# One plain tile of gate and up instead of two at the front of each feed-forward layer, with the sums of x chained

## The chip, the cores and the metric

The program runs on one core of one Trainium2 chip. The core has a matrix engine (TensorE, "PE" in the rows; "PEld" is its loading of the stationary operand), a vector engine (VectorE, "DVE"), a scalar engine (ScalarE, "ACT"), a general engine (GpSimd, "POOL") and a queue engine (SyncE, "SP"). Each takes its instructions in a fixed order that was settled when the program was built. The metric is the device time of one execution in microseconds. Before the change it is 2099.26 us, the median of 3 runs (2099.06 to 2102.05).

## The reference

Two residual layers over a (1, 1024, 1024) stream, every sub-layer behind an RMSNorm. The even layer mixes by a short convolution and an mLSTM, the odd layer by a gated MLP over chunks. Each of the two ends in a SwiGLU feed-forward with D_MODEL = 1024 and D_FF = 2816, and that is where the change lies:

```python
def swiglu(xn, w_in, w_out):
    h = xn @ w_in
    g, up = h[..., :D_FF], h[..., D_FF:]
    return (jax.nn.silu(g) * up) @ w_out

# in each layer
x = x + mixer(rmsnorm(x, norm_mix[layer]), ...)
x = x + swiglu(rmsnorm(x, norm_ffn[layer]), ffn_w_in[layer], ffn_w_out[layer])
```

## The kernel before

Activations lie transposed: 8 blocks d of 128 features by two halves c of 512 tokens, in float32. Every product is made in three passes of TensorE (`mm3`, L121 to L123): each operand is cut into a rounded part (h) and the remainder (l), and h·h, h·l and l·h are added up. A cut costs one cast on ACT (L96 for x, L110 or L329 for weights) and one subtraction on DVE (L97, L111, L330).

The hidden layer has NF = 22 tiles f of 128 features, each with a gate and an up part. They are computed in two ways.

- The first DIRECT = 2 tiles are **plain** (`direct`, L429 on): for each half c of the tokens `project` runs gate and up over all 8 blocks, 48 matmuls of 128x512 per tile and half. The tiles of PSUM are called f0g and f0u in layer 0, f1g and f1u in layer 1.
- The other tiles are made **by quarters** (`Halves`, `blocks`, `into`): the gate and up weights of a tile are one row of blocks a11, a12, a21, a22, x is cut into four blocks by feature half and token half, and seven products in the manner of Winograd replace eight. A unit is one tile; its seven products have 12 matmuls each, 84 in all, into three banks A, B and C of PSUM (Af0i, Bf0i, Cf0i). The order of the products is fixed in `STEPS`: a11·b11, a12·b21, s2·t2, s1·t1, s3·t3, s4·b22, a22·t4. The weights' own sums (s1 to s4, L340 to L343) come out of DVE and are cut as hix/lox (s2, s4), hiy/loy (s1, a22) and hiz/loz (s3); a11 and a12 are hia/loa.

On the side of x, b11 is feature blocks 0 to 3 of token half 0, b21 blocks 4 to 7 of half 0, and b22 blocks 4 to 7 of half 1; all three are there already as the cut x that the plain tiles use. The four sums t1 to t4 are not. They are made by adding DMAs on the POOL queue (`gather`, L394: the destination in SBUF is added to, 256 KB each, in place in the float32 x), four blocks each, `mix_x`, and then cut on ACT and DVE, `cut_x`. So there are 16 gathers per layer. In the names of the rows xe (layer 0) and xo (layer 1) is the float32 x; x_ffn01*k*h and x_ffn01*k*l is block k of token half 1 after scaling and cutting; f0t1*k*h is the rounded part of block k of t1.

The second half of x is not ready when the layer starts. The mixer's output projection ends with half 1; then TensorE sums the squares (ss_ffn, L162), DVE makes the root (L166 to L190) and a diagonal matrix of it (dg_ffn, L175), TensorE spreads that over the partitions (r_ffn, L179), ACT copies it to SBUF (L244), and DVE scales the eight blocks (L248), each of which is then cut (L96, L97). Only after the scaling of a block may a gather read it.

The program is written in one sequence; a list scheduler at build time decides from it, by priorities and its own costs, the order on each engine. Pools set limits: 4 staging buffers for weights (`wst`), 4 for the rounded and 4 for the remainder parts (`whl`), 5 + 3 banks of PSUM. The generator `blocks` loads and cuts the first unit's weights step by step, one step for each `next(run)`; the steps of `swiglu` that call it lie at L581 to L596.

Of the kernel before, what the change touches and what calls it, by code (L numbers as in the profile page):

```python
# [25 lines left out]
EPS = 1e-6  # L26
PAIRS = (2, 2, 2, 3)
TAIL = 4
DIRECT = 2
GELU_C = math.sqrt(2.0 / math.pi)  # L30
GELU_A = 0.044715
BIG = 1e30
# [11 lines left out]
def trunk(ctx, tc, x_t, vecs, b_gate, b_s, ws_t, we, we_v, we_g, we_o, wo_u, wo_v, wo_o, wf_in, wf_out, out_t):  # L44
# [48 lines left out]
    def split(src, name):  # L93
        hi = slot(f"{name}h", F32R)
        lo = slot(f"{name}l", F32R)
        nc.scalar.copy(hi[:, :HALF], src)  # L96
        nc.vector.tensor_tensor(lo[:, :HALF], src, hi[:, :HALF].bitcast(F32), op=ALU.subtract)  # L97
        return hi, lo
# [264 lines left out]
    def blocks(units):  # L363

        w = units[0][0]
        w.load()
        yield
        w.rows()
        yield
        w.sums()  # L370
        yield
        w.below()
        w.third()
        yield
        for i, (w, xb, sink, then) in enumerate(units):
            ahead = units[i + 1][0] if i + 1 < len(units) else None
            if ahead:
                ahead.load()
            banks = {"a": acc(f"A{w.name}"), "b": acc(f"B{w.name}"), "c": misc(f"C{w.name}")}
            for s, (wn, xn, bank, first) in enumerate(STEPS):  # L380
                wh, wl = w.get(wn)
                ps = banks[bank]
                nt = w.n // P
                for k in range(nt):
                    cols = slice(k * P, (k + 1) * P)
                    xh, xl = xb[xn][k]
                    mm3(ps, (wh[:, cols], wl[:, cols]), (xh[:, :HALF], xl[:, :HALF]), first and k == 0, k == nt - 1, not first)
                sink(s, ps)
                if ahead and s in (1, 4, 5, 6):
                    {1: ahead.rows, 4: ahead.sums, 5: ahead.below, 6: ahead.third}[s]()  # L390
                then(s)

    def gather(dst, src):
        nc.gpsimd.dma_start(dst, src, accum_op=ALU.add)  # L394

    def swiglu(layer, normed, todo, spans, after):
# [19 lines left out]
        def settle(f):  # L416

            if f >= NF - TAIL:
                for c in range(2):
                    store(hs.pop((f, c)), td[f - NF + TAIL], c, f"{name}h{f}{c}")  # L420
            elif f % 2:
                x11, x12, x21, x22 = (hs.pop((ff, c)) for ff in (f - 1, f) for c in range(2))
                for b, t in (("b11", x11), ("b21", x21), ("b22", x22)):
                    store(t, hd[f // 2], BLOCKS.index(b), f"{name}h{f}{b}")
                for b, t, more in (("t1", x11, x12), ("t3", x12, x22), ("t2", x22, x11), ("t4", x21, x22)):
                    nc.vector.tensor_tensor(t, t, more, op=ALU.add)
                    store(t, hd[f // 2], BLOCKS.index(b), f"{name}h{f}{b}")

        def direct(f):  # L429
            wg = weights(wf_in[layer, f], f"{name}g{f}")  # L430
            wu = weights(wf_in[layer, NF + f], f"{name}u{f}")

            def job(c):
                pg = project(wg, xs, c, f"{name}g{f}{c}")
                pu = project(wu, xs, c, f"{name}u{f}{c}")
                hs[f, c] = gate(pg, pu, f, c)

            return job

        def into(f):  # L440
            st = {}

            def sink(s, ps):
# [23 lines left out]
                else:  # L467
                    r = st["r"]
                    nc.vector.scalar_tensor_tensor(r, r, 0.5, ps, op0=ALU.mult, op1=ALU.mult)
                    hs[f, 0] = r  # L470
                    if f == DIRECT:
                        settle(f - 1)
# [11 lines left out]
        def onto(dp, ch):  # L484
            opening = ch == 0
            rows, hold = (2 * dp, 2 * dp + 1), {}

            def add(d, c, t):
                to = x[d][c][:, :HALF]
                nc.vector.tensor_tensor(to, t, to, op=ALU.add)  # L490

            def keep(d, c, ps):
                t = slot(f"{name}x{d}{c}" if opening else f"{name}e{d}{c}")
                if opening:
                    x[d][c] = t
                hold[d, c] = t[:, :HALF]
                nc.scalar.copy(hold[d, c], ps)

            def less(d, c, p, q):
                nc.vector.tensor_tensor(hold[d, c], p, q, op=ALU.subtract)  # L500
                if not opening:
                    gather(x[d][c][:, :HALF], hold[d, c])

            def sink(s, ps):
                d0, d1 = rows
                if s in (0, 6) and opening:
                    keep(d0 if s == 0 else d1, 0, ps)
                elif s in (0, 1, 6):
                    add(d1 if s == 6 else d0, 0, ps)
                elif s in (2, 3):  # L510
                    keep(d0 if s == 2 else d1, 1, ps)
                elif s == 4:
                    less(d1, 1, hold[d1, 1], ps)
                else:
                    less(d0, 1, ps, hold[d0, 1])
                if s == 6 and ch == len(PAIRS) - 1:
                    for d in rows:
                        for c in range(2):
                            gather(x[d][c][:, :HALF], x_in[d * P : (d + 1) * P, c * HALF : (c + 1) * HALF])

            return sink
# [19 lines left out]
        def early(ch, todo):  # L541
            def then(s):
                for i in todo.get(s, ()):
                    bring(ch, i)

            return then

        units, xb = [], {b: [] for b in BLOCKS}
        for f in range(DIRECT, NF):
            w = Halves(wf_in[layer, f], wf_in[layer, NF + f], HALF, f"{name}i{f}")  # L550
# [4 lines left out]
        for ch, n in enumerate(PAIRS):  # L555
            for dp in range(4):
                w2 = [wf_out[layer, base + i * P * n * 256 : base + (i + 1) * P * n * 256].rearrange("(p x) -> p x", p=P) for i in range(2)]
                base += 2 * P * n * 256
                units.append((Halves(w2[0], w2[1], n * P, f"{name}o{ch}{dp}"), hbs[ch], onto(dp, ch), early(ch + 1, (spread if ch < len(PAIRS) - 1 else ending)[dp])))
        jobs = [direct(f) for f in range(DIRECT)]  # L560
        jobs[0](0)
# [2 lines left out]
        for b, d0, c in (("b11", 0, 0), ("b21", 4, 0), ("b22", 4, 1)):  # L564
            xb[b] = [xs[d0 + k][c] for k in range(4)]

        mixes = (("t1", 0, 0, 0, 1), ("t3", 0, 1, 4, 1), ("t2", 4, 1, 0, 0), ("t4", 4, 0, 4, 1))

        def mix_x(b):
            for bb, d0, c, d1, cc in mixes:  # L570
                for k in range(4):
                    if bb == b:
                        gather(xf[d0 + k][c], xf[d1 + k][cc])

        def cut_x(b):
            for bb, d0, c, _, _ in mixes:
                for k in range(4):
                    if bb == b:
                        xb[b].append(split(xf[d0 + k][c], f"{name}{b}{k}"))

        run = blocks(units)  # L581
        next(run)
        for b, *_ in mixes:
            mix_x(b)
        jobs[1](0)
        cut_x("t1")
        jobs[0](1)
        next(run)
        cut_x("t3")
        cut_x("t2")  # L590
        next(run)
        jobs[1](1)
        next(run)
        cut_x("t4")
        for _ in run:
# [489 lines left out]
    n1, n2, n3 = Scaled("ffn0"), Norm("mix1", True, spill), Scaled("ffn1")  # L1085
    x, todo = even(n1)
    x, todo = swiglu(0, n1, todo, halves, n2)
    x, todo = odd(n2, todo, n3)
    x, todo = swiglu(1, n3, todo, thirds, Final())
    for step in todo:  # L1090
        step()
# [60 lines left out]
```

## Time and profile before

| | |
|---|---|
| median of 3 runs | 2099.26 us |
| profiled execution | 2099.18 us |
| its span, first to last instruction | 2097.5 us |
| outside the span | 1.7 us |
| TensorE busy | 2075.4 us, 99% |
| VectorE busy | 1376.9 us, 66% |
| ScalarE busy | 825.0 us, 39% |
| GpSimd busy | 277.2 us, 13% |
| mean granted clock of TensorE | 0.996 of full speed |

A row of the timeline gives the start from the span's beginning, the duration, engine, line, operation, the tile written and the tiles read, with a count where equal rows were merged; in brackets stands the idle time of that engine before it and what ended it. Matmuls overlap, so the pace of a run of them is the distance of their starts and not their duration; the same holds for ACT and DVE, whose next instruction can start some 0.1 us before the last one's end.

### The profile page before, as it was taken

How to read it: one execution, taken by the hardware profiler on the slowest of the kernel's cores; microseconds unless marked ns; L12 is line 12 of the kernel's file. 1: busy time of each engine (PE TensorE's matmuls, PEld its weight loads, DVE VectorE, ACT ScalarE, POOL GpSimd, SP SyncE). 2: the span in 40 equal slices, each digit the busy share in tenths (PEclk: the TensorE clock that was granted, in tenths of full speed). 3: DMA queues.
4: the chain of work that ended last, by engine and by line, in shares of the span. 5: the costliest groups of instructions: out<-in, count | busy, mean ns of one | idle time of the engine just before them, and what ended most of it. 6: DMA issues, size and time to landing. Idle time of an engine off the chain costs nothing.

```text
span 2097.5 us, 25504 instructions
## 1 busy us (share of the span) xinstructions
PE 2075.4 (99%) x9294; PEld 1680.6 (80%) x9294; DVE 1376.9 (66%) x2176; ACT 825.0 (39%) x1277; POOL 277.2 (13%) x453
## 2 busy tenths in 40 slices
PE   9999999999999999999999999999999999999998
PEld 7878888888888878877778888888888888877777
DVE  6236566568877777666556666666877777656566
ACT  5111112345444444343235743445444444433234
POOL 0000000003222121101231000002212112001120
PEclk9999999999999999999999999999999999999999
DMA  5121111545444344479994221445534434379993
GB/s 172 61 76 61 46 51 51 189 142 122 179 152 160 131 158 157 156 279 277 309 253 158 91 71 41 169 158 116 184 128 161 160 126 169 114 273 306 322 231 97
DMA packets 131935, 327.89 MB, mean 156 GB/s; under 512 B 17073, under 2 KB 19153, under 8 KB 131809
## 3 DMA queue, kind: packets, MB, share of 16 engines
q1 hardware_dynamic: 88912, 209.77, 29.2%
q0 software_dynamic: 42752, 116.46, 19.2%
q8 instruction: 73, 1.20, 0.2%
q14 instruction: 54, 0.43, 0.1%
q10 hardware_dynamic: 144, 0.03, 0.0%
HBM read 213.98 MB, written 91.24 MB: 146 GB/s over the span
## 4 chain that ended last, share of the span: by engine, by line
PE 89%; issue 5%; DMA 4%; DVE 1%; POOL 1%; ACT 0%; SPq 0%; DVEq 0%; POOLq 0%; ACTq 0%
PE Af1i L121 4%; PE Af1i L122 4%; PE Af1i L123 4%; PE Af0i L121 2%; PE Af0i L122 2%; PE Af0i L123 2%; PE Bf1i L121 2%; PE Bf1i L123 2%; PE Bf1i L122 2%; PE Af1o L121 2%; PE Af1o L123 1%; PE Af1o L122 1%; PE ov L121 1%; PE op L121 1%; PE ou L121 1%
## 5 line engine op out<-in xcount | busy, mean ns | idle before, releaser
L260 POOL DMA_DIRECT2D x_dram<-xe x16 | 8.6, 540 | 450.8 <-DVE xe L274 445.7
L260 POOL DMA_DIRECT2D x_dram<-xo x16 | 8.6, 540 | 276.8 <-DVE xo L274 271.7
L110 ACT CAST hi_eo<-st_eo 128x1024 fp32r<-128x1024 f32 x20 | 21.0, 1049 | 48.9 <-PE ep L122 30.6
L459 DVE TENSOR_TENSOR f0q<-f0q,Af0i 128x512 f32<-128x512 f32 x20 | 13.8, 688 | 35.9 <-PE Af0i L123 35.9
L459 DVE TENSOR_TENSOR f1q<-f1q,Af1i 128x512 f32<-128x512 f32 x20 | 13.7, 687 | 35.7 <-PE Af1i L123 35.7
L394 POOL DMA_DIRECT2D f0x<-f0e x24 | 20.7, 874 | 120.3 <-DVE f0e L500 103.7
L394 POOL DMA_DIRECT2D f1x<-f1e x24 | 21.0, 878 | 117.9 <-DVE f1e L500 95.3
L329 ACT CAST hix_f0i<-st_f0i 128x1024 fp32r<-128x1024 f32 x20 | 21.1, 1053 | 39.2 <-PE Af0i L122 25.1
L329 ACT CAST hix_f1i<-st_f1i 128x1024 fp32r<-128x1024 f32 x20 | 21.0, 1052 | 38.5 <-PE Af1i L122 25.1
L329 ACT CAST hiy_f1i<-st_f1i 128x1024 fp32r<-128x1024 f32 x20 | 21.1, 1053 | 31.3 <-PE Bf1i L122 30.7
L329 ACT CAST hiy_f0i<-st_f0i 128x1024 fp32r<-128x1024 f32 x20 | 21.1, 1055 | 31.1 <-PE Bf0i L122 30.6
L449 DVE TENSOR_TENSOR f1b<-Cf1i,f1b 128x512 f32<-128x512 f32 x20 | 13.8, 689 | 26.6 <-issue 17.9
L449 DVE TENSOR_TENSOR f0b<-Cf0i,f0b 128x512 f32<-128x512 f32 x20 | 13.8, 688 | 26.6 <-issue 17.9
L121 PE MATMUL f1y<-f1h,hi_f1o 128*128 128x256 f32 (+1 forms) x96 | 30.8, 321 | 0.0
L122 PE MATMUL f1y<-f1h,hi_f1o 128*128 128x256 f32 (+1 forms) x96 | 30.8, 321 | 0.0
L110 ACT CAST hi_oo<-st_oo 128x1024 fp32r<-128x1024 f32 x16 | 16.8, 1052 | 35.1 <-PE op L122 26.9
L123 PE MATMUL f1y<-f1h,lo_f1o 128*128 128x256 f32 (+1 forms) x96 | 30.6, 319 | 0.0
L110 ACT CAST hi_evw<-st_evw 128x1024 fp32r<-128x1024 f32 x8 | 8.4, 1050 | 55.5 <-PE ek L122 36.6
L329 ACT CAST hia_f1i<-st_f1i 128x1024 fp32r<-128x1024 f32 x20 | 21.0, 1050 | 22.2 <-PE Cf1i L122 18.4
L329 ACT CAST hia_f0i<-st_f0i 128x1024 fp32r<-128x1024 f32 x20 | 21.0, 1049 | 22.2 <-PE Cf0i L122 18.4
L111 DVE TENSOR_TENSOR lo_eo<-st_eo,hi_eo 128x1024 fp32r<-128x1024 f32 x20 | 24.5, 1223 | 7.5 <-ACT hi_eo L110 7.5
L274 DVE TENSOR_TENSOR xe<-ep,xe 128x512 f32<-128x512 f32 x16 | 11.0, 690 | 27.5 <-PE ep L123 27.4
(3189 smaller groups left out, 7405.5 us busy)
## 6 DMA issues: line engine op xcount, KB each, us to landing
f0h<-hd SPq DMA_DIRECT2D x126, 256.0 KB, 5.8
f1h<-hd SPq DMA_DIRECT2D x126, 256.0 KB, 5.8
st_f0i<-wf_in SPq DMA_DIRECT2D x40, 512.0 KB, 3.5
st_f1i<-wf_in SPq DMA_DIRECT2D x40, 512.0 KB, 3.4
st_eo<-we_o SPq DMA_DIRECT2D x16, 512.0 KB, 3.7
st_oo<-wo_o SPq DMA_DIRECT2D x16, 512.0 KB, 3.5
st_f0o<-wf_out SPq DMA_DIRECT2D x24, 256.0 KB, 3.5
f0x<-f0e POOLq DMA_DIRECT2D x24, 256.0 KB, 6.6
```

The source lines that it names most:

```text
L110: nc.scalar.copy(hi[:, part], st[:, part])
L111: nc.vector.tensor_tensor(lo[:, part], st[:, part], hi[:, part].bitcast(F32), op=ALU.subtract)
L121: nc.tensor.matmul(ps, lhsT=lh, rhs=rh, start=first, stop=False, skip_group_check=more)
L122: nc.tensor.matmul(ps, lhsT=lh, rhs=rl, start=False, stop=False, skip_group_check=more)
L123: nc.tensor.matmul(ps, lhsT=ll, rhs=rh, start=False, stop=last, skip_group_check=more)
L260: nc.gpsimd.dma_start(x_at[0][d * P : (d + 1) * P, c * HALF : (c + 1) * HALF], x[d][c][:, :HALF])
L274: nc.vector.tensor_tensor(x, ps, x, op=ALU.add)
L329: nc.scalar.copy(hi, src)
L394: nc.gpsimd.dma_start(dst, src, accum_op=ALU.add)
L449: nc.vector.tensor_tensor(r, ps, r, op=ALU.add)
L459: nc.vector.tensor_tensor(st["q"], st["q"], ps, op=ALU.subtract)
```

## The change

DIRECT goes from 2 to 1: tile 1 becomes a unit by quarters, so that each layer has 21 units in place of 20. The sums of x are chained in another way. Write x00 for feature blocks 0 to 3 of half 0, x40 for blocks 4 to 7 of half 0, x01 and x41 for the same of half 1. Before, t2 was made in the place of x41 by adding t1, and t4 in the place of x40 by adding t2; now t2 is made on top of t1 (in the place of x00) by adding x41, and t4 again by adding t2 to x40. So t1 must be cut before t2 may be added over it, and the calls of `mix_x` and `cut_x` are interleaved with what is left of the plain tile and with the steps of `blocks`.

```diff
-DIRECT = 2
+DIRECT = 1
...
-        mixes = (("t1", 0, 0, 0, 1), ("t3", 0, 1, 4, 1), ("t2", 4, 1, 0, 0), ("t4", 4, 0, 4, 1))
+        mixes = (("t1", 0, 0, 0, 1), ("t3", 0, 1, 4, 1), ("t2", 0, 0, 4, 1), ("t4", 4, 0, 0, 0))
...
         run = blocks(units)
         next(run)
-        for b, *_ in mixes:
-            mix_x(b)
-        jobs[1](0)
+        mix_x("t1")
+        mix_x("t3")
         cut_x("t1")
+        mix_x("t2")
+        next(run)
         jobs[0](1)
-        next(run)
-        cut_x("t3")
         cut_x("t2")
         next(run)
-        jobs[1](1)
+        mix_x("t4")
+        cut_x("t3")
         next(run)
         cut_x("t4")
```

What this does to the order on the engines is shown at three places of layer 0; layer 1 has the same order.

**TensorE, from the sums of squares of half 1 on, before.** f0g_3602 is the gate of the second plain tile over half 0, r_ffn the spread root:

```order
L123 MATMUL f0u_3487<-x_ffn007h,lo_f0u_86_3446 128x512
L162 MATMUL ss_ffn_3519<-ones,tot_ffn_3098 128x1 x4
L121 MATMUL f0g_3602<-x_ffn000h,hi_f0g_87_3451 128x512
L122 MATMUL f0g_3602<-x_ffn000l,hi_f0g_87_3451 128x512
L123 MATMUL f0g_3602<-x_ffn000h,lo_f0g_87_3452 128x512
L121 MATMUL f0g_3602<-x_ffn001h,hi_f0g_87_3451 128x512
```

The same place now, with f0g_3606 the one plain tile over half 1 and Cf0i_49 the second product of the first unit:

```order
L123 MATMUL f0u_3475<-x_ffn007h,lo_f0u_87_3446 128x512
L162 MATMUL ss_ffn_3507<-ones,tot_ffn_3098 128x1 x4
L179 MATMUL r_ffn_3524<-dg_ffn_3519,ones 128x128 x4
L121 MATMUL Cf0i_49_3736<-x_ffn004h,hia_f0i_49_3602 128x512
L122 MATMUL Cf0i_49_3736<-x_ffn004l,hia_f0i_49_3602 128x512
L123 MATMUL Cf0i_49_3736<-x_ffn004h,loa_f0i_49_3603 128x512
L121 MATMUL Cf0i_49_3736<-x_ffn005h,hia_f0i_49_3602 128x512
L122 MATMUL Cf0i_49_3736<-x_ffn005l,hia_f0i_49_3602 128x512
L123 MATMUL Cf0i_49_3736<-x_ffn005h,loa_f0i_49_3603 128x512
L121 MATMUL Cf0i_49_3736<-x_ffn006h,hia_f0i_49_3602 128x512
L121 MATMUL f0g_3606<-x_ffn010h,hi_f0g_86_3439 128x512
```

Between the sums and the spread root stood 16 matmuls of the second plain tile; nothing stands there now, and half 1 of x is wanted 7 matmuls after the root where it was wanted after 32 more. From r_ffn to the first matmul of s1·t1 there are now 72 matmuls.

**GpSimd queue, the last eight gathers, before** (xe_3100, 3163, 3211 and 3259 are x41, xe_2754, 2756, 2758 and 2760 are x00, later t1, and xe_2797 to 2911 are x40):

```order
L394 DMA xe_3100<-xe_2754 128x512
L394 DMA xe_3163<-xe_2756 128x512
L394 DMA xe_3211<-xe_2758 128x512
L394 DMA xe_3259<-xe_2760 128x512
L394 DMA xe_2797<-xe_3100 128x512
L394 DMA xe_2835<-xe_3163 128x512
L394 DMA xe_2873<-xe_3211 128x512
L394 DMA xe_2911<-xe_3259 128x512
```

The same eight now:

```order
L394 DMA xe_2754<-xe_3100 128x512
L394 DMA xe_2756<-xe_3163 128x512
L394 DMA xe_2758<-xe_3211 128x512
L394 DMA xe_2797<-xe_2754 128x512
L394 DMA xe_2835<-xe_2756 128x512
L394 DMA xe_2760<-xe_3259 128x512
L394 DMA xe_2873<-xe_2758 128x512
L394 DMA xe_2911<-xe_2760 128x512
```

The fourth gather of t2 (onto xe_2760) now stands behind the first two of t4, which read what the first two of t2 have written.

**ScalarE, the cuts ahead of the first unit, before** (f0t2*k*h is the rounded part of block k of t2, hix and hiy those of the unit's weight sums):

```order
L96 CAST f0t20h<-xe_3100 128x512
L329 CAST hix_f0i_49_3769<-st_f0i_49_3582 128x1024
L96 CAST f0t21h<-xe_3163 128x512
L329 CAST hiy_f0i_49_3828<-st_f0i_49_3583 128x1024
L96 CAST f0t22h<-xe_3211 128x512
L405 ACTIVATE f0t_3823<-f0g_3773 128x512
L96 CAST f0t23h<-xe_3259 128x512
```

The same now:

```order
L96 CAST f0t13h<-xe_2760 128x512
L96 CAST f0t20h<-xe_2754 128x512
L96 CAST f0t21h<-xe_2756 128x512
L96 CAST f0t22h<-xe_2758 128x512
L329 CAST hix_f0i_49_3682<-st_f0i_49_3570 128x1024
L96 CAST f0t23h<-xe_2760 128x512
L329 CAST hiy_f0i_49_3706<-st_f0i_49_3571 128x1024
L96 CAST f0t30h<-xe_2949 128x512
L329 CAST hiz_f0i_49_3710<-s_f0i_49_3677 128x512
L329 CAST hia_f0i_50_3767<-st_f0i_50_3730 128x1024
```

The cut of s1 (hiy) and that of the next unit's a11 (hia_f0i_50) now stand behind all four casts of t2.

## Rows read from the trace of the kernel before

**Rows 1.** The page: span and busy time, then the chain that ended last.
```profile
span 2097.5 us, 25504 instructions
...
PE 2075.4 (99%) x9294; PEld 1680.6 (80%) x9294; DVE 1376.9 (66%) x2176; ACT 825.0 (39%) x1277; POOL 277.2 (13%) x453
...
PE 89%; issue 5%; DMA 4%; DVE 1%; POOL 1%; ACT 0%; SPq 0%; DVEq 0%; POOLq 0%; ACTq 0%
```

**Rows 2.** Timeline of PE, layer 0, sums of squares to the spread root.
```profile
472.02 0.95 PE L162 MATMUL ss_ffn<-ones,tot_ffn 128*128 128x1 f32 x8
472.83 0.47 PE L121 MATMUL f0g<-x_ffn000h,hi_f0g 128*128 128x512 f32 x1
...
476.64 1.05 PE L179 MATMUL r_ffn<-dg_ffn,ones 128*128 128x128 f32 x8
477.45 0.48 PE L122 MATMUL f0g<-x_ffn005l,hi_f0g 128*128 128x512 f32 x1
```

**Rows 3.** Timeline of PE, first and last start of a run of 72 matmuls.
```profile
490.50 0.40 PE L121 MATMUL f0u<-x_ffn010h,hi_f0u 128*128 128x512 f32 x1
...
507.22 0.39 PE L121 MATMUL Af0i<-x_ffn000h,hia_f0i 128*128 128x512 f32 x1
```

**Rows 4.** Timeline of DVE, layer 0: root, scaling and cuts of half 1.
```profile
474.31 0.87 DVE L175 TENSOR_SCALAR dg_ffn<-ident,col_ffn 128x128 f32<-128x128 f32 x4
478.35 2.08 DVE L248 SCALAR_TENSOR_TENSOR xe<-xe,vec,r_ffn 128x512 f32<-128x512 f32 x3 [3.17 <-ACT r_ffn L244]
480.34 0.69 DVE L97 TENSOR_TENSOR x_ffn010l<-xe,x_ffn010h 128x512 fp32r<-128x512 f32 x1
...
482.27 0.69 DVE L97 TENSOR_TENSOR x_ffn011l<-xe,x_ffn011h 128x512 fp32r<-128x512 f32 x1
...
487.88 0.69 DVE L97 TENSOR_TENSOR x_ffn017l<-xe,x_ffn017h 128x512 fp32r<-128x512 f32 x1
488.48 0.68 DVE L406 SCALAR_TENSOR_TENSOR f0b<-f0t,f0g 128x512 f32<-128x512 f32 x1
...
502.70 1.23 DVE L330 TENSOR_TENSOR loy_f0i<-st_f0i,hiy_f0i 128x1024 fp32r<-128x1024 f32 x1 [0.30 <-ACT hiy_f0i L329]
```

**Rows 5.** Timeline of ACT, layer 0: casts of x, of t1 and of s1.
```profile
479.14 0.62 ACT L96 CAST x_ffn010h<-xe 128x512 fp32r<-128x512 f32 x1 [0.82 <-DVE xe L248]
...
486.71 0.62 ACT L96 CAST f0t10h<-xe 128x512 fp32r<-128x512 f32 x1
487.23 0.61 ACT L96 CAST f0t11h<-xe 128x512 fp32r<-128x512 f32 x1
...
501.62 1.05 ACT L329 CAST hiy_f0i<-st_f0i 128x1024 fp32r<-128x1024 f32 x1 [0.57 <-PE f0g L122]
```

**Rows 6.** Timeline of POOL, layer 0: fourth gather of t2 with first of t4, then t4.
```profile
494.48 1.74 POOL L394 DMA_DIRECT2D xe<-xe  x2 [1.03 <-DVE s_f0i L340]
496.48 0.86 POOL L394 DMA_DIRECT2D xe<-xe  x1 [0.26 <-DMA xe<-xe]
...
499.51 0.86 POOL L394 DMA_DIRECT2D xe<-xe  x1 [0.71 <-DMA xe<-xe]
```

**Rows 7.** Windows of the gathers: engines' busy time, PEclk, DMA share, GB/s; layers 0, 1.
```profile
479.66:505.00 25.34, 25.34 (x111) 20.52 (x110) 24.44 (x38) 17.00 (x29) 13.85 (x16) 1.00 1.02 178
1434.50:1460.00 25.50, 25.50 (x111) 20.60 (x110) 24.54 (x38) 17.23 (x29) 13.87 (x16) 1.00 1.00 165
```

**Rows 8.** DMA issues 470 to 530 us: queue, count, KB, us to landing.
```profile
xe<-xe POOLq DMA_DIRECT2D x16, 256.0 KB, 5.2
...
hd<-f0h1b11h POOLq DMA_DIRECT2D x1, 256.0 KB, 2.3
```

**Rows 9.** Tile f0t10h, layer 0: when its product with s1 runs.
```profile
L121 PE MATMUL Bf0i<-f0t10h,hiy_f0i x1: 397/397/397, 515.6 to 515.6; 128*128 128x512 f32 x1
```

**Rows 10.** Windows at the end of the span, columns as in Rows 7.
```profile
2089.00:2090.00 1.00, 0.00 (x0) 0.00 (x0) 0.79 (x5) 0.04 (x1) 0.00 (x0) 1.00 0.00 0
...
2091.00:2092.00 1.00, 0.07 (x1) 0.00 (x0) 0.89 (x2) 0.00 (x0) 0.00 (x0) 0.50 0.00 0
```

## The prediction

> **What bounds the kernel now.** I read the page first: TensorE is busy for 99% of the span, VectorE for 66% and ScalarE for 39% [rows 1]. So what counts is how many matmuls there are and whether anything makes TensorE wait. Then I read TensorE's timeline where the change lies, at the front of a feed-forward layer: 72 starts of 128x512 matmuls take 507.22 - 490.50 = 16.72 us, 0.232 us each, without a gap [rows 3]. The sums of squares, 15 to 16 matmuls of the second plain tile and the spread root follow each other without a gap too [rows 2]. Next I followed what half 1 of x goes through beside that: VectorE finishes the diagonal of the root at 474.31 + 0.87 = 475.18, the scaling starts at 478.35 after ScalarE's copy, and the last block is cut from 487.88 on, with the next VectorE instruction 0.60 later [rows 4]. ScalarE's casts stand 0.52 apart [rows 5]. Last come the gathers: during the 25.3 us of the sixteen the DMA engines are full (share 1.02, in layer 1 1.00) [rows 7], and one takes 5.2 us to land in the median [rows 8]. None of this shows, because TensorE works on plain tiles meanwhile: the cast of t1 that was made at 486.71 [rows 5] is used by s1·t1 at 515.6 [rows 9]. That is the cover which the change thins out.
>
> **What goes.** A plain tile costs 96 matmuls over both halves, a unit by quarters 84. So 12 matmuls go per layer: 12 x 0.232 = 2.8 us per layer, 5.6 us in all, all of it on the path. ScalarE and VectorE get one more unit (casts, subtractions and sums, some 8 us on VectorE); at 66% they carry that beside the matmuls, and I count it as nothing except where they queue behind a wait, below.
>
> **What is moved, layer 0.** I carry the new order forward with the durations of the rows.
>
> (a) Sums to root. Before, the next matmul after the sums starts at 472.83, and the root takes 477.45 - 476.64 = 0.81 of TensorE's time amid plain matmuls [rows 2]. Now nothing stands between them, so TensorE waits for the diagonal. The fourth part of it is there at 475.18, so the root ends at about 475.6 and the next matmul starts at 475.4. Without a wait that would be 472.83 + 0.81 = 473.64: a wait of 1.8 us. Since the root ended at 476.64 + 1.05 = 477.69 before, all scaling, cutting and the first gathers come 2.1 us earlier.
>
> (b) Half 1 is wanted at once. Seven matmuls of a12·b21 last to 477.0. The cast of block 0 ends at 479.14 + 0.62 - 2.1 = 477.7, its remainder at 480.34 + 0.69 - 2.1 = 478.9, that of block 1 at 482.27 + 0.69 - 2.1 = 480.9. Between these stand 5 and 6 matmuls; the waits are 0.6, 0.1 and 0.55, together 1.25 us. After that the matmuls are slower than the cuts. So the 72 matmuls from the root to s1·t1 end at 475.4 + 16.7 + 1.25 = 493.4.
>
> (c) s1·t1 needs hiy, the cut of s1 on ScalarE. It stands behind all four casts of t2 there, and the fourth cast needs the fourth gather of t2, which in turn stands on the POOL queue behind two gathers of t4 that wait for t2's first and second. The last cut of x starts at 487.88 - 2.1 = 485.8; the subtractions for t1's blocks 0 and 1 follow at 0.60 each and end at 487.1 and 487.7. Only then may t2 be added over t1: the issues of its first two gathers start at about 487.4 and 488.25 (0.86 each on POOL [rows 6]). The second one's landing is the tenth of the layer. Before, the gather that waits for it starts at 496.48 [rows 6]; the DMA engines are full up to there in either order, so I take 496.48 - 2.1 = 494.4 for t4's second gather. POOL is free for t2's fourth at 495.3. From an issue to the start of the gather that needs it I take 499.51 - 494.48 = 5.0 [rows 6]: landed at 500.3. Then a cast (0.52), then hiy (1.05 [rows 5]), ready at 502.0. TensorE has been idle from 493.4: 8.6 us.
>
> The Trainium skill puts another price on a gather: its page "DMA: Bandwidth & Descriptors", section "Anatomy of one DMA", gives about 2.0 us fixed plus the bytes over 436 GB/s, which for 256 KB is an estimate of 2.6 us. This trace does not agree while the queue is full (median 5.2 [rows 8]). By the page's price for the two landings in the chain the waits would be some 4 us shorter per layer, near the first rival below.
>
> (d) The third matmul of s1·t1 needs loy, 1.23 on VectorE behind hiy [rows 4], ready at 503.2 against 502.5: 0.75. The next unit's a11 is cut behind that in the same queues (three subtractions at 0.60 and one of 1.23): ready at 506.3 against 506.1, 0.2. Further on the rows of order leave VectorE some slack again; I count nothing.
>
> (e) The clock. At the end of the span TensorE does nothing from 2089 to 2090 and next to nothing from 2091 on; between the two the granted clock goes from 1.00 to 0.50, from 2.4 to 1.2 GHz [rows 10]; so after 8.6 us of idling I expect the lower level. How long it stays is not in the trace. Bounds: nothing, or one whole product of 12 matmuls at half speed, 12 x 0.232 = 2.8 us more. There is no row nearer to either, so I take the middle, 1.5.
>
> The sum per layer: -2.8 + 1.8 + 1.25 + 8.6 + 0.75 + 0.2 + 1.5 = +11.3. Layer 1 has the same order and gathers at the same pace [rows 7], so +22.6. On the profiled execution (span 2097.5 and 1.7 around it, 2099.18, which is 0.1 under the median of the runs) that gives 2099.2 + 22.6 = 2121.8; I say 2122.
>
> **Rivals.**
>
> *The gathers land sooner.* The queue may be emptier late in the chain than it was before. The fastest landing from POOL in this stretch is 2.3 us after its issue [rows 8], a plain store. Then t2's second lands at 488.25 + 0.86 + 2.3 = 491.4, t2's fourth is issued by 493.1 and lands at 495.4, hiy is ready at 497.0, and (c) is 3.6. With no loss by the clock: -2.8 + 1.8 + 1.25 + 3.6 + 0.95 = +4.8 per layer, 2109. For it: the last gathers of t2 and t4 wait for one another, so fewer are in flight. Against: the first eight gathers are queued as before, and a share of 1.0 says that the engines, not the waits, set the pace.
>
> *The delay spreads.* Some thirty cuts on VectorE and ScalarE are queued behind the late casts of t2, the next unit's among them. If a gather takes 6 us instead of 5, or if the weights of the third unit are cut too late as well because their staging buffers come free late, then each of the next two units waits again. Two landings 1 us longer are 2 us, the clock's upper bound 1.3 more, two late cuts at 0.8 (as in (d)) 1.6: +5 per layer, 2132. For it: by (d) the next unit's cut has no slack. Against: VectorE has a third of its time free.
>
> *The matmuls decide (faster).* If the scheduling leaves TensorE fed, only the 12 matmuls per layer count: 2099.2 - 5.6 = 2093.6. It decides when the waits of (a) to (d) are under 2.8 us per layer, which wants hiy by about 493 and the root without a wait. Against: (a) and (b) alone are 3.05 by measured durations, and hiy by 493 would need two gathers in sequence after 488.25 to land in no time. That the matmuls don't go at all can be left out: the order has 24 fewer rows on TensorE.
>
> *No change:* the waits come to just the 2.8 saved. The same reasons speak against it.
>
> The Trainium skill's page "TensorE: Matmul & The Clock Gate", section "The HAM clock gate", says that the array's clock is halved by default and that sustained work releases it. Rows 10 agree with the fall; what the return costs no row here shows, and by this rule (e) is not zero.
>
> **How the numbers follow.** The forecast has 0.70, the sooner landings 0.10, the spreading delay 0.15, faster 0.03, no change 0.02. The forecast's own range takes in the clock's bounds (1.4 either way per layer) and 2 us of landing time per layer: 2115 to 2129. The range from 2108 to 2134 takes in the two slower cases and leaves out the others. A measurement of this kernel tells about 0.2% (4.2 us) from no change; by the cases slower than that has 0.95, within 0.02, faster 0.03.
>
> **What would show it.** In the profile after: TensorE idle ahead of the root, released by the diagonal, near 2 us; some 9 us ahead of the first matmul on hiy in each layer, released by ScalarE's cast; ScalarE idle ahead of the casts of t2, released by a gather; PEclk at 0.5 for a while behind it; 24 fewer matmuls. I am wrong if TensorE's idle time near 475 to 505 is under 5 us per layer, or if the gathers of t2 land within 3 us.

## The result, and the profile after

| | before | after |
|---|---|---|
| median of the runs | 2100.36 us (4 runs, 2099.06 to 2102.05) | 2130.53 us (4 runs, 2127.19 to 2132.19) |
| profiled execution | 2099.18 us | 2129.52 us |
| its span | 2097.5 us | 2127.6 us |
| mean granted clock | 0.996 | 0.989 |

After stands to before as 1.0142 (95% interval 1.0127 to 1.0157): slower by 30 us where 22.6 had been forecast. That is within the whole range (2108 to 2134), but 1.5 us above the forecast's own part of it (2115 to 2129), on the side of the rival of the spreading delay (2132). The page of the changed kernel answers to [rows 1]: 24 matmuls fewer, and TensorE's share has gone from 99% to 98%.

```profile
span 2127.6 us, 25476 instructions
...
PE 2080.8 (98%) x9270; PEld 1682.3 (79%) x9270; DVE 1392.4 (65%) x2194; ACT 832.4 (39%) x1287; POOL 277.6 (13%) x453
```

TensorE's waits of the whole span (who, for whom: us in total, times, the longest) name the places at once. Of those shown here the kernel before has only the one for x001h, with 0.7:

```profile
PE Bf0i L121 <- ACT hiy_f0i L329: 8.5, 1, 8.5
PE Bf1i L121 <- ACT hiy_f1i L329: 8.4, 1, 8.4
PE r_ffn L179 <- DVE dg_ffn L175: 3.5, 2, 1.8
PE eq L121 <- ACT x001h L195: 2.7, 1, 2.7
...
PE f0g L121 <- ACT x_ffn010h L96: 0.5, 1, 0.5
```

TensorE's timeline of layer 0 answers to [rows 2, 3, 9]. Watch the starts: behind the waits of 1.76 and 0.49 they come 0.23 apart for most of the way up to 496.63, then there is nothing for 8.54, then they come 0.43 apart until 511.26.

```profile
475.61 0.95 PE L162 MATMUL ss_ffn<-ones,tot_ffn 128*128 128x1 f32 x8
478.32 1.13 PE L179 MATMUL r_ffn<-dg_ffn,ones 128*128 128x128 f32 x8 [1.76 <-DVE dg_ffn L175]
...
480.68 0.40 PE L121 MATMUL Cf0i<-x_ffn006h,hia_f0i 128*128 128x512 f32 x1
481.57 0.50 PE L121 MATMUL f0g<-x_ffn010h,hi_f0g 128*128 128x512 f32 x1 [0.49 <-ACT x_ffn010h L96]
...
496.63 0.40 PE L123 MATMUL Cf0i<-x_ffn007h,loa_f0i 128*128 128x512 f32 x1
505.57 0.80 PE L121 MATMUL Bf0i<-f0t10h,hiy_f0i 128*128 128x512 f32 x1 [8.54 <-ACT hiy_f0i L329]
506.16 0.63 PE L122 MATMUL Bf0i<-f0t10l,hiy_f0i 128*128 128x512 f32 x1
506.83 0.80 PE L123 MATMUL Bf0i<-f0t10h,loy_f0i 128*128 128x512 f32 x1
507.42 0.63 PE L121 MATMUL Bf0i<-f0t11h,hiy_f0i 128*128 128x512 f32 x1
507.85 0.63 PE L122 MATMUL Bf0i<-f0t11l,hiy_f0i 128*128 128x512 f32 x1
...
511.26 0.39 PE L121 MATMUL Af0i<-x_ffn000h,hia_f0i 128*128 128x512 f32 x1
```

ScalarE's timeline shows why, and answers to [rows 5]: hiy stands behind the fourth cast of t2, which waits for a landing.

```profile
496.90 0.62 ACT L96 CAST f0t20h<-xe 128x512 fp32r<-128x512 f32 x1 [3.76 <-DMA xe<-xe]
...
503.95 0.62 ACT L96 CAST f0t23h<-xe 128x512 fp32r<-128x512 f32 x1 [2.76 <-DMA xe<-xe]
504.48 1.04 ACT L329 CAST hiy_f0i<-st_f0i 128x1024 fp32r<-128x1024 f32 x1
```

GpSimd's timeline answers to [rows 6]: the gather at 497.17 is t4's first, which waits for t2's first; t2's fourth is the second of the three from 498.43 on. The second fence has the gathers' windows in layers 0 and 1, which answer to [rows 7], and the row of the DMA issues, which answers to [rows 8]:

```profile
497.17 0.86 POOL L394 DMA_DIRECT2D xe<-xe  x1 [2.58 <-DMA xe<-xe]
498.43 2.63 POOL L394 DMA_DIRECT2D xe<-xe  x3 [0.41 <-DMA xe<-xe]
```

```profile
481.42:507.00 25.58, 16.86 (x68) 12.73 (x69) 20.42 (x32) 14.34 (x23) 13.96 (x16) 0.88 1.01 180
1448.50:1474.00 25.50, 17.11 (x71) 13.54 (x70) 20.10 (x32) 13.83 (x22) 13.92 (x16) 0.90 0.97 167
...
xe<-xe POOLq DMA_DIRECT2D x16, 256.0 KB, 5.2
```

Windows of layer 0 show the clock (columns as in [rows 7]; the clock is the third last); they answer to [rows 10]:

```profile
500.00:501.00 1.00, 0.00 (x0) 0.00 (x0) 0.81 (x2) 0.94 (x2) 1.00 (x2) 1.00 1.02 174
501.00:502.00 1.00, 0.00 (x0) 0.00 (x0) 0.78 (x1) 0.19 (x1) 0.06 (x1) 0.50 1.10 191
510.00:511.00 1.00, 1.00 (x4) 0.81 (x3) 1.00 (x2) 1.00 (x3) 0.00 (x0) 0.50 0.06 25
```

For the whole front and the units of a layer I use one measure below, "the front": from the first start of the first plain product to the first start of the down projection. TensorE's timeline has both, here of before and then of after, layer 0:

```profile
460.93 0.40 PE L121 MATMUL f0g<-x_ffn000h,hi_f0g 128*128 128x512 f32 x1
...
897.34 0.39 PE L121 MATMUL Af0o<-f0h,hia_f0o 128*128 128x512 f32 x1
```

```profile
464.52 0.40 PE L121 MATMUL f0g<-x_ffn000h,hi_f0g 128*128 128x512 f32 x1
...
913.82 0.40 PE L121 MATMUL Af0o<-f0h,hia_f0o 128*128 128x512 f32 x1
```

That is 436.4 before and 449.3 after: +12.9; in layer 1, in the same way, 436.4 and 448.5: +12.2. The 30.1 us between the two spans are then 3.6 at the start of the kernel (464.52 against 460.93), 12.9, -0.3 up to layer 1, 12.2, and 1.8 behind it. The 3.6 are not the change's: TensorE's order up to there is the same in both kernels, and the difference is made in the first 15 us. TensorE waited 2.7 for x001h in this execution in place of 0.7 (up to 2.8 in those of the experiments), and behind that the granted clock was 0.50 from 9.60 to 14.60 in place of 1.00. The kernels of the experiments reach the front anywhere from 460.75 (run 2) to 464.31 (run 4).

### The profile page after: what moved, and what is told of

Its sections match the earlier page's. It is cut to its first block, busy times and chain, and to the rows that moved or that the text cites. A ratio compares the mean times of both kernels' runs of the same rounds, so it can differ in the third digit from the quotient of the medians.

```text
span 2127.6 us, 25476 instructions
## 1 busy us (share of the span) xinstructions
PE 2080.8 (98%) x9270; PEld 1682.3 (79%) x9270; DVE 1392.4 (65%) x2194; ACT 832.4 (39%) x1287; POOL 277.6 (13%) x453
## 4 chain that ended last, share of the span: by engine, by line
PE 90%; DMA 4%; issue 2%; DVE 2%; ACT 1%; POOL 1%; SPq 0%; DVEq 0%; ACTq 0%; POOLq 0%
PE Af0i L121 4%; PE Af0i L122 4%; PE Af0i L123 4%; PE Af1i L121 3%; PE Af1i L122 3%; PE Af1i L123 3%; PE Bf0i L123 2%; PE Bf0i L121 2%; PE Bf0i L122 2%; PE Bf1i L121 2%; PE Bf1i L123 2%; PE Bf1i L122 2%; PE op L121 1%; PE ep L121 1%; PE ep L122 1%
## 5 line engine op out<-in xcount | busy, mean ns | idle before, releaser
L260 POOL DMA_DIRECT2D x_dram<-xe x16 | 8.6, 540 | 454.4 <-DVE xe L274 449.3
```

Of the source, the lines that this page charges most:

```text
L260: nc.gpsimd.dma_start(x_at[0][d * P : (d + 1) * P, c * HALF : (c + 1) * HALF], x[d][c][:, :HALF])
```

## The experiments

The time given is the median; in brackets is the ratio to the kernel before on the same chip, with its 95% interval. "Front" gives what the front is longer than before's 436.4, in layers 0 and 1. Where an edit adds lines, the line numbers behind it are higher.

**1. The plain tile alone** (the order and calls of the sums as before):

```diff
-mixes = (("t1", 0, 0, 0, 1), ("t3", 0, 1, 4, 1), ("t2", 0, 0, 4, 1), ("t4", 4, 0, 0, 0))
+mixes = (("t1", 0, 0, 0, 1), ("t3", 0, 1, 4, 1), ("t2", 4, 1, 0, 0), ("t4", 4, 0, 4, 1))
...
+for b, *_ in mixes:
+    mix_x(b)
+cut_x("t1"); jobs[0](1); next(run); cut_x("t3"); cut_x("t2"); next(run); next(run); cut_x("t4")
```

> Part one alone: one plain tile at the front, but the sums of x as before (t2 and t4 are added onto half 1 of x, none reads what another has just had cut). TensorE's order up to s1*t1 is that of the changed kernel; on ScalarE the cast of s1 (hiy) now stands behind the cast of one block of t2 in place of four. Theory (the chain t1, t2, t4 through GpSimd's queue and ScalarE's order holds hiy back): the waits for the root and for half 1, together 2.9 us per layer, stay; the wait for hiy falls from 8.5 to 1 to 3 us; with 12 matmuls fewer (2.8 us) that is +1 to +4 per layer, 2102 to 2108, and no stretch at 1.2 GHz. Rival (the missing plain tile alone costs it, whatever the order of the sums): wait for hiy near 8.5 as in the changed kernel, 2125 to 2130.

Measured 2126.59 us (1.0122, 1.0108 to 1.0137, an interval that overlaps that of the changed kernel); front +11.8, +10.9. A miss: the wait for hiy fell to the upper end of what was expected, but hardly any time came back, and the rival's time came out. The waits of TensorE:

```profile
PE r_ffn L179 <- DVE dg_ffn L175: 3.5, 2, 1.8
PE Bf1i L121 <- ACT hiy_f1i L329: 3.2, 1, 3.2
PE Bf0i L121 <- ACT hiy_f0i L329: 3.0, 1, 3.0
...
PE Af0i L121 <- ACT f0b L446: 2.3, 1, 2.3
PE Af1i L121 <- ACT f1b L446: 1.9, 1, 1.9
```

f0b at L446 is the copy that empties bank A after the first product. It stands behind the last cast of t4 on ScalarE, and so behind the sixteenth gather:

```profile
508.25 0.62 ACT L96 CAST f0t43h<-xe 128x512 fp32r<-128x512 f32 x1 [1.45 <-DMA xe<-xe]
508.77 0.58 ACT L446 COPY f0b<-Af0i 128x512 f32<-128x512 f32 x1
```

And s1·t1 ran at 1.2 GHz here too, behind a wait of only 3 us. In layer 0 the matmuls behind the root did so as well (granted clock 0.51 from 476.70 to 480.20), which in the changed kernel they did not (1.00 from 478.30 to 480.70): part of what the shorter wait gave back went to the clock.

**2. The chained sums alone** (the changed kernel with `DIRECT = 2`, `jobs[1](0)` behind `mix_x("t3")` and `jobs[1](1)` behind `cut_x("t3")`).

> Part two alone: two plain tiles as before, but the sums chained through the first quarter's tiles as in the changed kernel. Theory: 32 to 36 plain matmuls (about 8 us) lie between root and s1*t1 that the changed kernel has not, so the late hiy is hidden: no wait over 0.5 us ahead of s1*t1, 2097 to 2102, as before. Rival (the chain alone costs it, as the gathers land later and later however much work stands beside them): a wait for hiy of 4 us or more per layer, 2107 or above.

Measured 2101.35 us (1.0000, 0.9991 to 1.0009); front -0.7, +0.2. As the theory had it: beside two plain tiles the chain costs nothing that these runs can tell.

**3. The weights' cuts first:**

```diff
 jobs[0](1)
+next(run); next(run)
 cut_x("t2")
-next(run)
 mix_x("t4"); cut_x("t3")
-next(run)
 cut_x("t4")
```

> The changed kernel, with the cuts of the first unit's weight sums handed out ahead of the cuts of t2: on ScalarE hix, hiy and hiz stand behind one cast of t2 in place of four; gathers and TensorE's order up to s1*t1 are unchanged. Theory (order of ScalarE's queue): the first cast of t2 started at 496.9 in the changed kernel, so hiy is ready near 499.5 in place of 505.5; wait 2.5 per layer in place of 8.5, no or little time at 1.2 GHz; per layer -2.8 + 2.9 + 2.5 + 0.5 = +3, 2103 to 2109. Rival (the gathers or the missing cover are what counts, so the wait only moves to the next product that needs x): the sum of the waits per layer stays over 8 us, 2120 or above.

Measured 2122.52 us (1.0102, 1.0088 to 1.0116); front +8.9, +9.6. A miss again, and the rival's time came out, with waits of 7.5 and 8.2 per layer (it had said over 8), although hiy was early: 1.8 and 2.1 for hiy, 0.7 for loy, 2.5 and 2.4 for f0b and f1b, 0.7 for their next copies, 1.8 for the root, 0.5 for half 1 in layer 1, and low clock around the root in layer 0 and in s1·t1 of layer 1.

**4. t2 and t4 added by VectorE** (`nc.vector.tensor_tensor(to, to, more, op=ALU.add)` for these two in place of the gathers).

> The changed kernel, with t2 and t4 added by VectorE in place of eight accumulating gathers; ScalarE's order keeps hiy behind all four casts of t2 and one of t3. Theory (the landings of t2 hold the casts, the casts hold hiy): the four casts of t2 no longer wait for a landing; hiy is ready by 496 to 498 and the wait ahead of s1*t1 is 0 to 1 us, no time at 1.2 GHz; what stays is the root and half 1 of x, 2.9 per layer, against 2.8 saved: 2098 to 2103. Rival (position in ScalarE's queue alone, or VectorE as the new bound, with eight sums more at 0.6 us each): a wait of 4 us or more for hiy or loy per layer, 2110 or above.

Measured 2127.40 us (1.0131, 1.0115 to 1.0147, so not told apart from the changed kernel); front +12.5, +11.4. The rival came true. The wait for hiy was 5.6 and 4.9. ScalarE's timeline shows hix ahead of it waiting for VectorE's weight sums, and the windows show VectorE (the third busy time) with no gap:

```profile
500.36 1.05 ACT L329 CAST hix_f0i<-st_f0i 128x1024 fp32r<-128x1024 f32 x1 [3.07 <-DVE st_f0i L343]
501.31 1.04 ACT L329 CAST hiy_f0i<-st_f0i 128x1024 fp32r<-128x1024 f32 x1
```

```profile
490.00:495.00 5.00, 5.00 (x23) 4.06 (x22) 5.00 (x10) 4.47 (x7) 0.86 (x1) 1.00 0.89 156
495.00:500.00 5.00, 1.82 (x8) 1.13 (x6) 5.00 (x9) 1.14 (x2) 0.00 (x0) 1.00 0.00 0
```

After four runs my theory had fallen as a statement on one chain. As I read the waits of these runs, ScalarE's order, the gathers and VectorE's amount of work end close to one another, and taking one away shows the next. What they share is that they start at the root. In the changed kernel that is at 475.61, though VectorE ends the last sum of squares at 466.17 + 0.69 = 466.86: the sums stand behind the whole plain tile. So the second theory: the time from the sums to s1·t1 is some 30 us (505.57 - 475.61 = 29.96 in the changed kernel, 24 to 27 in runs 1, 3 and 4, where other waits follow), and what counts above all is how many matmuls stand beside it.

**5. The clock kept up** by 28 matmuls behind the second product of the first unit, which read the first block of t2 and whose result nothing reads. To place them there, `blocks` yields once more behind that product, which also moves the copy f0b on ScalarE ahead of the casts of t4 and changes TensorE's order behind s1·t1; so the edit is not the matmuls alone.

> The changed kernel with 28 matmuls more per layer, whose result nothing reads, in the wait ahead of s1*t1; they start when the first block of t2 is cut (near 497.5) and take 28 x 0.232 = 6.5 us there, so TensorE is busy until s1 is cut (505.5). Theory (the clock costs apart from the wait: 12 matmuls of s1*t1 at 0.427 in place of 0.232, 2.3 us per layer): s1*t1 runs at 0.232 each and the whole comes out 2 to 2.5 us per layer under the changed kernel, 2124 to 2127. Rival (the products behind s1*t1 wait for late cuts of t2, t3 and t4 on ScalarE and VectorE anyway, so what the clock gives back is waited away): no difference from the changed kernel, 2128 to 2132.

Measured 2124.50 us (1.0113, 1.0099 to 1.0127); front +11.3, +10.7. In TensorE's timeline s1·t1 runs at 0.23 per matmul behind them:

```profile
494.63 6.82 PE L599 MATMUL f0idle<-f0t20h,hia_f0i 128*128 128x512 f32 x28 [0.34 <-ACT f0t20h L96]
502.69 0.50 PE L121 MATMUL Bf0i<-f0t10h,hiy_f0i 128*128 128x512 f32 x1 [1.24 <-ACT hiy_f0i L329]
...
504.29 0.40 PE L121 MATMUL Bf0i<-f0t11h,hiy_f0i 128*128 128x512 f32 x1
...
506.37 0.40 PE L121 MATMUL Af0i<-x_ffn000h,hia_f0i 128*128 128x512 f32 x1
```

So with 28 matmuls more in each layer the kernel was faster: every one of its runs lies under every one of the changed kernel's, though the intervals of the ratios just touch. Of the 6 us between the medians the two fronts hold 1.6 + 1.5 = 3.1; the rest is in the parts that both have, as the 3.6 above. s1·t1 itself takes 506.37 - 502.69 = 3.68 in place of 5.69, and in layer 0 its end comes 45.31 us into the front in place of 46.74: 1.4 of the 1.6 are gained there, ahead of everything that the other order touches on TensorE. In layer 1 the end comes at 45.53 in place of 46.40, 0.9 of 1.5. The remainder may come from the moved copy, which no run separates.

**6. The early root** in the changed kernel:

```diff
-jobs[0](0)
 for step in todo:
     step()
+jobs[0](0)
```

> The changed kernel with the sums and the root of half 1 ahead of the plain tile's first half in the order (they then stand behind 10 of its 48 matmuls; the last of the sums of squares was ready at 463.8, and the sums ran at 475.6 in the changed kernel). Nothing else is changed. Theory (from root to s1*t1 the chain through VectorE, ScalarE and the gathers takes 475.6 to 505.5 = 30 us, and TensorE has only 72 matmuls and the root, 18.5 us, to do beside it): now 112 matmuls and the root, 27.8 us, stand there; the wait ahead of s1*t1 falls to about 2 us, the waits for the root and half 1 go, a wait of 0.5 for the last sum of squares comes; per layer -2.8 + 2.1 + 0.5 with 0 to 1.5 for the clock: 2097 to 2102. Rival (VectorE's amount of work, or the weights, set the end of that chain, not when it starts): wait still over 6 us per layer, 2118 or above.

Measured 2110.54 us (1.0048, 1.0034 to 1.0061); front +5.0, +4.0. Two thirds of the loss went by moving the root alone: the sums ran 2.5 us into the front (463.71 against 461.23) in place of 11.1. Of the expectation the wait for hiy (2.8 and 2.7 for 2) was close, the sum was not: s1·t1 still ran at 1.2 GHz, in layer 0 nearly all of it, in layer 1 its first half. These waits and the clock come to 3.2 of the 5.0 in layer 0 (2.8 + 0.8 for hiy and loy, 2.4 for the clock, 2.8 saved); the rest I have not traced.

**7. Early root and weights' cuts first** (the edits of 6 and 3).

> The early root of the run before, and the cuts of the first unit's weight sums handed out ahead of those of t2 as in the third run. Theory: the chain is some 6 us shorter still, so that the 27.8 us of matmuls cover it; the later waits of that third run (2.5 for the second unit's sinks) are covered by the 8 us that the root moved up. What stays is 0.5 for the last sum of squares against 12 matmuls saved: 2093 to 2097, faster than both kernels. Rival (a front with one plain tile has VectorE full for 35 us, which shows as waits further on whatever the order): waits of 2 us or more per layer among the first three units, 2098 or above.

Measured 2104.03 us (1.0015, 1.0006 to 1.0023); front +0.7, +2.8. Short of the expectation, and the time is the rival's: 1.3 and 1.8 remain ahead of t2's product, again for the copy f0b behind the last cast of t4, and 0.4 for the next copy.

**8. Control: the kernel before with the early root** (the edit of 6 on it).

> Control: the kernel before, two plain tiles and its own sums, with the early root alone. Theory (with two plain tiles the chain is covered already, TensorE waits nowhere in that stretch): 2098 to 2102, the same as before, a wait of at most 0.5 us for the last sum of squares. Rival (the early root is a gain by itself, through emptier queues): 2096 or below.

Measured 2102.07 us (1.0004, 0.9995 to 1.0012); front 0.0, +0.4. The early root is worth nothing where two plain tiles cover the chain.

**9. Early sums of the weights, chained sums of x.** Beside the early root, `run` is begun and advanced by three steps ahead of it, and `blocks` yields after the second product of the first unit, so that `cut_x("t3")` and `cut_x("t4")` are handed out behind the copy of the first.

> One plain tile, early root, chained sums; beside that the sums of the first unit's weights and the cut of s2 are handed out ahead of the root, so that VectorE makes them while it still waits for the mixer (it was full from 469 to 499 in the early-root run), and the copy of the first unit's first product goes to ScalarE ahead of the casts of t3 and t4. Theory (too little of VectorE's and ScalarE's work lies beside plain matmuls): no wait over 1 us in the first three units; 12 matmuls saved against 0.4 us more around the root, -2.4 per layer: 2094 to 2098, faster than both kernels. Rival (the landings of the chained gathers are the bound that is left): a wait of 1.5 us or more per layer for t2 or t4, 2099 or above.

Measured 2105.48 us (1.0019, 1.0010 to 1.0028); front +1.0, +1.2. The rival: TensorE waits 2.8 and 2.5 for f0b and f1b, which ScalarE reaches only behind t2's casts, and all four of those wait for landings (the last two are shown):

```profile
492.71 0.62 ACT L96 CAST f0t22h<-xe 128x512 fp32r<-128x512 f32 x1 [1.98 <-DMA xe<-xe]
494.13 0.62 ACT L96 CAST f0t23h<-xe 128x512 fp32r<-128x512 f32 x1 [0.80 <-DMA xe<-xe]
494.65 0.58 ACT L448 COPY f0b<-Af0i 128x512 f32<-128x512 f32 x1
```

**10. The same with the sums of x as before** (the `mixes` of 1).

> As the run before, with the sums of x as in the kernel before (t2 and t4 added onto half 1) in place of the chained ones. Theory: the chaining has cost or gained next to nothing so far (the plain tile alone and the whole change were 4 us apart, the chain alone and the kernel before 0.6): within 3 us of the run before, 2094 to 2100. Rival (the chaining matters once the cover is short): 4 us or more from the run before, by a wait for t2's or t4's landing in one of the two.

Measured 2100.27 us (0.9994, 0.9986 to 1.0003); front -1.1, +0.1. 5.2 us under run 9, where at most 3 had been expected, so the rival holds: the wait for f0b is 0.9 and 0.6 here. That is not the chaining alone: the order of the calls goes with it, and t3's casts, which run 9 has behind f0b, stand ahead of t2's here, whose waits for landings are 0.93 and 0.65 in layer 0. No run separates the two, and run 11 is faster with the chained sums.

**11. Copy first.** The kernel of 7, with the yield of 9 ahead of `cut_x("t4")` alone:

```diff
                 sink(s, ps)
+                if i == 0 and s == 1:
+                    yield
...
 cut_x("t3")
+next(run)
 cut_x("t4")
```

> The early root with the weights' cuts first, as run before, and only the copy of the first unit's first product moved on ScalarE, ahead of the casts of t4. Theory (that run was left with 1.3 and 1.8 us of waiting for this copy, which stood behind the last cast of t4 and so behind the sixteenth gather): those waits go, 1.5 to 2.5 us per layer with what the clock took: 2099 to 2102. Rival (the wait goes to t2's product or to the copy's successor): same as that run, 2103 to 2106.

Measured 2097.91 us (0.9980, 0.9971 to 0.9988); front -2.1, -1.4. Better than expected, and this beats both kernels, the one before by 0.2% and the changed one by about 1.5% (2097.9 to 2130.5). TensorE's timeline has the root amid plain matmuls, and nothing waits over 0.5 us in the first units:

```profile
466.27 1.13 PE L179 MATMUL r_ffn<-dg_ffn,ones 128*128 128x128 f32 x8
467.15 0.48 PE L123 MATMUL f0g<-x_ffn005h,lo_f0g 128*128 128x512 f32 x1
```

**12. Control: the kernel of 11 with the root back behind the plain tile.**

> Control to the run that is faster than both kernels: all of its order, weights' cuts first and the copy of the first product ahead of t4's casts, but the sums and the root of half 1 back behind the whole plain tile, as in the changed kernel. Theory (when the root comes is what counts; the order of ScalarE only decides where the wait shows): of the third run's 2122.5 the two waits of 2.4 for that copy go or move to the next product that needs a late cut: 2116 to 2122, still 7 or more per layer over the kernel before. Rival (the order of ScalarE alone does it, the early root is not needed): 2105 or below.

Measured 2118.25 us (1.0088, 1.0070 to 1.0106); front +8.7, +9.6. As the theory had it. ScalarE's order without the early root gives 12 of the 33 us between the changed kernel and run 11, the early root on top of it the other 20.

## Why the prediction was right, and where it was not

The sign, the place and the mechanism held: TensorE lost its time in the waits and the slow stretch that (a) to (e) name; the front lost 12.9 and 12.2 where 11.3 was forecast. By its steps, layer 0:

- What goes: the page counts 24 matmuls fewer, at the pace of [rows 3]. Right, and run 11 shows that they are worth something once nothing waits: its fronts are 2.1 and 1.4 us shorter than before's, of the 2.8 counted.
- (a) The wait for the root: 1.76 (layer 1: 1.77) for 1.8. Right.
- (b) Half 1: one wait of 0.49 in place of three with 1.25 together. Too high: the order was the one forecast, with 5 and 6 matmuls between, but VectorE scaled one block between the remainders of blocks 0 and 1 where it had scaled two before, so that block 1's was ready at 483.37 + 0.69 - 3.6 = 480.5 in place of 480.9, and the wait of 0.55 for it fell away.
- (c) The wait for hiy: 8.54 (8.4) for 8.6. Less the 3.6 of the late start, hiy is ready at 505.5 - 3.6 = 501.9 (forecast 502.0) and TensorE idle from 505.57 - 8.54 - 3.6 = 493.4 (forecast 493.4). A gather still took 5.2 in the median. The Trainium skill's page "DMA: Bandwidth & Descriptors", section "Anatomy of one DMA", gives some 2.0 us fixed plus the bytes over 436 GB/s, from which 2.6 us is an estimate for this size; the trace after does not agree either, with 5.2 us at a DMA share of 1.01.
- (d) 0.95 for loy and loa was too high: the third matmul of s1·t1 starts 506.83 - 506.16 = 0.67 behind the second, where 0.43 is the pace there: 0.24.
- (e) The clock, 1.5, is the term that was mis-sized. The 12 matmuls of s1·t1 take 511.26 - 505.57 = 5.69; less 0.24 for loy and less 12 x 0.232 that is 2.7, just under the upper bound of 2.8. In layer 1 they take 4.74, by the same count 1.7, but there another stretch at 1.2 GHz followed the wait of (a), 1.4 more, which the forecast had not counted (below). Run 5 bears the term out: with TensorE busy through the wait the 12 take 3.68.

These come to -2.8 + 1.76 + 0.49 + 8.54 + 0.24 + 2.7 = 10.9 of 12.9. The idle times in brackets leave out that the first matmuls behind a wait start further apart than 0.23 (481.57 to 481.90, for one). Counted by starts, (a) to (c) are 505.57 - 475.61 less the sums and the root (0.81 each) and 72 x 0.232 = 16.7, which is 11.6; the forecast had 1.8 + 1.25 + 8.6 = 11.65. That this agrees so well is in part luck, as (b) was too high by what (a) and (c) were too low. So 0.8 of the missing 2.0 lie ahead of s1·t1, and the other 1.1 lie behind it, in pieces that I have not traced. Of the miss of 7.5 us on the execution, 2.5 are the fronts', 3.6 come from the kernel's start and 1.8 from its end.

What the prediction did not see is how little of the loss goes when hiy comes sooner. It put 8.6 of the 11.3 on the wait for hiy, and I expected runs 1, 3 and 4 to give most of it back; by the medians they gave 4, 8 and 3 us, and only the 8 are clear of the intervals. As those runs read, the wait was the first to show of three that end close together. Which instruction TensorE waits for says what comes last, not what it would cost to be without it; run 6, which shortens nothing and only starts everything earlier, gave 20.

Of the rivals, the sooner landings had no part in it: two gathers in sequence took what the forecast gave them (t2's fourth cast starts at 503.95 - 3.6 = 500.35, forecast 500.3). The spreading delay has nearly the measured time, but not by its mechanism: behind s1·t1 the changed kernel has no wait over 0.2 us for a late cut or copy in the next units. It is true of runs 1, 3, 7 and 9 (the copy f0b) more than of the changed kernel itself.

## What to carry to other kernels

Work that seems to do nothing but its own arithmetic may be the cover of a chain on other engines: before thinning it, measure the chain from its first to its last instruction and count what matmuls are left beside it. When several queues wait for one event, move the event and not the queues: here the reduction stood behind 38 matmuls that it had no need of. After that, look again for what stands between a late transfer and an instruction that TensorE needs on the same in-order engine (here a copy of 0.58 us behind a cast that waited for the last gather).

## What the runs showed of the hardware that was not expected

The same wait of TensorE left the clock up in one layer and took it down in the other. Both layers of the changed kernel wait 1.8 us ahead of the root, behind the eight matmuls of the sums. In layer 0 the matmuls behind the root start 0.23 to 0.31 apart, and the seventh starts 480.68 - 478.32 = 2.36 behind the root. In layer 1 they start 0.43 apart and the seventh 1449.60 - 1445.81 = 3.79 behind it, 1.4 us more, as TensorE's timeline and a window there show (clock third last):

```profile
1445.81 1.43 PE L179 MATMUL r_ffn<-dg_ffn,ones 128*128 128x128 f32 x8 [1.77 <-DVE dg_ffn L175]
1446.89 0.78 PE L121 MATMUL Cf1i<-x_ffn104h,hia_f1i 128*128 128x512 f32 x1
...
1449.60 0.54 PE L121 MATMUL Cf1i<-x_ffn106h,hia_f1i 128*128 128x512 f32 x1
```

```profile
1445.80:1449.00 3.20, 3.19 (x13) 2.81 (x14) 1.55 (x5) 0.91 (x2) 0.00 (x0) 0.61 0.00 0
```

It is not the layer that decides: six kernels have this wait of 1.8 us (the changed one and runs 1, 3, 4, 5 and 12), twelve times in all, and behind eight of these the matmuls at first start 0.43 apart, in runs 1 and 5 in both layers, and behind the other four they don't. In the same way the wait of 2.8 us in layer 0 of run 9 cost nothing further, while nearly all 12 matmuls of s1·t1 were slow behind that of 3.0 us in layer 0 of run 1 and that of 2.8 us in layer 0 of run 6. Waits of this size had either price here, and a forecast needs both as its bounds.
